# A matmul with batch norm on one core: a raw block and a DMA-turned block more, and the order of the work written out as a table

## Chip, core and metric

The kernel runs on one core of a Trainium2 chip. The metric is the device time of one execution in microseconds. The kernel before takes 205.89 us, the median of three runs (205.88 to 206.04). All times below are microseconds unless they are marked ns. The five engines are PE (TensorE), DVE (VectorE), ACT (ScalarE), POOL (GpSimd) and SP (SyncE, which here only issues DMAs).

## What is computed

```python
y = np.matmul(x, weight)            # x 16 x 512 x 1024, weight 1024 x 768, float32
mean = np.mean(y, axis=(0, 1), keepdims=True)
var = np.var(y, axis=(0, 1), keepdims=True)
y_norm = (y - mean) / np.sqrt(var + eps)
return (gamma * y_norm + beta).astype(np.float32)
```

Each of the 768 output columns is normalized over all 16 x 512 = 8192 rows. No row of a column can be stored before the sums over all 8192 rows of this column are known.

## The kernel before

**Tiling.** The rows form C = 16 chunks of 512 rows, numbered c. The columns form six tiles of 128, numbered nt = 0 to 5. "Fourth tile" is nt = 3, "fifth tile" nt = 4, "sixth tile" nt = 5. The kernel has three stretches.

1. *Loading.* POOL issues DMAs that cast x to bfloat16 (L403). DVE turns the blocks so that the contraction dimension lies on the partitions (turn_x, L428 and L435). PE multiplies each chunk with the first two tiles, rows on the partitions (mm_rows, L510). ACT squares these, DVE and POOL add up sums and squares, ACT keeps the values in bfloat16. For chunks 0 to 3 PE also computes tiles 2 to 5 with the columns on the partitions (mm, L575). Some chunks are copied into a plain layout first (part_chunk, L547), on ACT or, for the last four, ACT or DVE.
2. *Turn-over.* Chunks 14 and 15 of the first two tiles are computed with columns on the partitions (ga_unit, L814). `merges` adds up the accumulators, `sums_rows` (L871) sums them over the partitions on PE, and scale and shift of the first two tiles follow (scale_rows, shift_rows, spread_rows L903). Between the loads and the first store lie "raw turns" (below).
3. *Output.* PE computes tiles 2 to 5 for chunks 4 to 15, tile by tile, while all finished blocks are normalized and stored. A tile's scale and shift come from finish_tasks (L968 to L1017), once all of its chunks have their sums.

**A column block.** Two chunks of one tile, 1024 rows, 512 KB of output. With the columns on the partitions it must be turned before it is stored. There are three ways:

- *pe* (col_block with MODE 'pe'): DVE normalizes it in place (norm, L1026), PE turns it with eight 128x128 transposes into PSUM (turn_block, L1044), ACT copies it to SBUF as float32 (L1210), SP stores it (L1202).
- *xact* (MODE 'xact'): the same norm, then SP issues a DMA that turns it (L1220), ACT converts the result to float32 (L1232), SP stores it (L1202).
- *raw* (RAW): SP turns the values before they are normalized (raw_turn, L1106, into the tile r_sb). When scale and shift are known, raw_spread makes rows of them (a DVE turn at L1142, gather and deal of small copies at L1145, a copy into a PSUM bank at L1158); DVE multiplies (norm_raw, L1174), POOL adds the shift (add_raw, L1178), SP stores (L1182). Raw turns of chunks 0 to 3 need no sums, so they may run ahead of the first store. The first of them waits for the last load of x.

In the kernel before, tile 2 has raw blocks c = 0 and 2 and 'xact' for the rest, the fourth tile raw c = 0 and 'xact' for the rest, the fifth tile raw c = 0, 2 and 4 and 'pe' for the rest. The last block of the fifth tile is held back (held_block, its norm early, its turn, copy L1252 and store L1255 after PE's last column matmul) to fill the time in which the sixth tile's sums are finished.

**The end.** The sixth tile's last chunk is computed in two pieces of 256 columns (last_unit, L753). Then follow the statistics of the last pieces (L760), the aggregate (L1308), the root on ACT (root, L1311) and the affine values on DVE (affine, L1323 and L1324). After them all 8192 rows of the sixth tile are normalized (norm_part, L1348), turned on PE, copied by ACT (L1361) and stored (L1364) in eleven blocks.

**What sets the order.** Every piece of work is a Task with a priority, the engines that may run it with occupation and latency, and what it depends on. arrange (L122 to L224) is a planner: it steps through time, picks the engine that is free first, and gives it the ready task of lowest priority number. A PE turn can be hosted by a matmul task: its transposes are issued between the matmuls. The instructions are emitted in this order and chained on each engine by `seq`, so each engine runs exactly its own sequence. SP too works in order: a store or turn that waits holds up all that are behind it.

negate_gamma (L963) makes -gamma for the scale of tile 2; it is one small DVE instruction (L964), after shift_rows.

Of the kernel before, what the change touches and what calls it, by code (L numbers as in the profile page):

```python
# [97 lines left out]
class Wires:  # L98
# [8 lines left out]
    def ready(self, queue):  # L107
        lanes = self.lanes[queue]
        return 0.0 if len(lanes) < self.LANES else lanes[-self.LANES]
# [9 lines left out]
        return t, land  # L119


def arrange(tasks, turns, log=None):  # L122

    free = {e: 1.25 for e in ("PE", "DVE", "ACT", "POOL", "SP")}
    wires = Wires()
    port = {"DVE": 0.0, "POOL": 0.0}
    left = sorted(tasks, key=lambda t: t.prio)
    order = []  # L130
    SEM, LOOK = 0.06, 0.2

    def ready(t):
        if t.after is not None and t.after.end is None:
            return None
        r = 0.0
        for d in t.deps:
            if d.end is None:
                return None
            r = max(r, d.end + SEM + t.slack)  # L140
        kept = [(s.pool, s.pool.mark()) for s in t.takes] if len(t.takes) > 1 else []
        fits = True
        for s in t.takes:
            p = s.pool.place(s)
            if p is None:
                fits = False
                break
            r = max(r, p[0] + SEM)
            if kept:
                s.pool.take(s, p[1])  # L150
        for pool, mark in reversed(kept):
            pool.reset(mark)
        if not fits:
            return None
        if t.dma:
            r = max(r, wires.ready(list(t.engines)[0]))
        return r

    def start_of(t, r, e):

        b = max(r, free[e])
        if e == "DVE" and t.lock:
            b = max(b, port["POOL"])
        elif e == "POOL" and not t.dma:
            b = max(b, port["DVE"])
        return b

    while left:
        seen = [(t, ready(t)) for t in left]
        first = {}  # L170
        for t, r in seen:
            if r is not None:
                for e in t.engines:
                    b = start_of(t, r, e)
                    if e not in first or b < first[e]:
                        first[e] = b
        if not first:
            raise RuntimeError(f"nothing can begin: {[(t.prio, t.emit) for t in left[:8]]}")
        e = min(first, key=lambda k: first[k])
        best = None  # L180
        for t, r in seen:
            if r is not None and e in t.engines and start_of(t, r, e) <= first[e] + max(LOOK, t.look):
                if best is None or t.prio < best[1]:
                    best = start_of(t, r, e), t.prio, t
        start, _, t = best
        for s in t.takes:
            s.pool.take(s, s.pool.place(s)[1])
        occ, lat = t.engines[e]
        t.hosted = []
        if t.hosts:  # L190
            room = t.hosts
            for u, r in seen:
                if u in turns and r is not None and r <= start + 0.3 and room >= 1:
                    n = min(room, turns[u][0])
                    if turns[u][0] == turns[u][1]:
                        places = [s.pool.place(s) for s in u.takes]
                        if any(p is None or p[0] > start for p in places):
                            continue
                        for s in u.takes:
                            s.pool.take(s, s.pool.place(s)[1])  # L200
                        u.takes_done, u.takes = u.takes, []
                    t.hosted.append((u, n))
                    turns[u][0] -= n
                    room -= n
                    occ += 0.0555 * n
                    lat += 0.0555 * n
        if t in turns:
            occ = lat = 0.0555 * turns[t][0]
            lat += 0.2
            t.count = turns[t][0]  # L210
        free[e] = start + occ
        if e == "DVE" and t.lock or e == "POOL" and not t.dma:
            port[e] = start + occ
        t.end = start + lat
        if t.dma:
            free[e], t.end = wires.send(e, start, occ, t.dma, t.count)
        t.start, t.engine = start, e
        order.append(t)
        left.remove(t)
        for u, n in t.hosted:  # L220
            if turns[u][0] == 0:
                u.end = t.end + 0.2
                left.remove(u)
    return order  # L224


# [1 line left out]
def kernel(  # L228
# [9 lines left out]
    nc = tc.nc  # L238
# [3 lines left out]
    ALU = mybir.AluOpType  # L242
# [5 lines left out]
    P = 128  # L248
# [24 lines left out]
    XT, YB, SQ = C - EARLY, 28, 3  # L273
    ADDED = (0,6,16,28,40)
    PARTED, LATE, SINGLE = (4,5,7,8,9,10), (12,13,14,15), (2,3,6)
    MODE = {2:'xact',3:'xact',4:('pe',)*8}
    MODE = {nt: m if isinstance(m, tuple) else (m,) * (C // GY) for nt, m in MODE.items()}
    RAW, RAWADD, RAWDUE = {2:(0,2),3:(0,),4:(0,2,4)}, {2:'POOL',3:'POOL',4:'POOL'}, {2:14.0,3:8.0,4:8.0}
    RING = 3 * CH // 32 * KQ // 2
    ENG = {"ACT": nc.scalar, "DVE": nc.vector, "POOL": nc.gpsimd, "SP": nc.sync}  # L280

# [11 lines left out]
    def seq(bi):  # L293

        ins = bi.ins
        prev = last.get(ins.engine)
        if prev is not None:
            tc.add_manual_dep(
                ins, prev,
                mybir.DependencyInfo(mybir.DependencyClass.NoSync, mybir.DependencyReason.DATA),  # L300
                reason="order",
            )
        last[ins.engine] = ins.name
        return bi

    gamma_sb = singles.tile([P, NT], f32)
# [28 lines left out]
    ngamma = singles.tile([P, NT], f32)  # L335
# [17 lines left out]
    tasks, turns = [], {}  # L353
    banks, xts, ys, sqs, rings = Pool(8), Pool(XT), Pool(YB), Pool(SQ), Space(RING)

    def task(prio, engines, emit, deps=(), lock=False, **kw):
        t = Task(prio, engines, emit, deps, **kw)
        t.lock = lock
        tasks.append(t)
        return t  # L360

    def dve(occ):
        return {"DVE": (occ, occ + 0.09)}

    def act(occ):
        return {"ACT": (occ, occ + 0.11)}

    def pool(occ):
        return {"POOL": (occ, occ + 0.05)}
# [70 lines left out]
    order = [("x", 0), ("w", 0, 2), ("x", 1), ("w", 2, 4)]  # L440
# [5 lines left out]
    t = 1.0  # L446
    affine = None
# [237 lines left out]
    def y_of(nt, c):  # L685
        return y_col.setdefault((nt, c // GY), Slot(ys))
# [174 lines left out]
    S = clock[0]  # L861
# [61 lines left out]
    sr = task(U + 0.1, dve(0.35), shift_rows, [sc], True)  # L923
# [32 lines left out]
    k = 0  # L956
# [4 lines left out]


    def negate_gamma(eng):  # L963
        seq(nc.vector.tensor_scalar(ngamma, gamma_sb, -1.0, None, op0=ALU.mult))  # L964

    ng = task(S, dve(0.1), negate_gamma, [affine, sr], True)

    def finish_tasks(nt):  # L968
        deps = [col_end[nt, c][0] for c in range(C)]
# [49 lines left out]
    def norm(nt, c, n=1):  # L1019
        def emit(eng):  # L1020
            part = y(nt, c, n)
            if eng == "ACT":
                seq(nc.scalar.activation(
                    part, part, AF.Identity, bias=shift[:, nt:nt + 1], scale=scale[:, nt:nt + 1]))
            else:
                seq(nc.vector.tensor_scalar(  # L1026
                    part, part, scale[:, nt:nt + 1], shift[:, nt:nt + 1],
                    op0=ALU.mult, op1=ALU.add))
        return emit
# [161 lines left out]
    def col_block(nt, c, due, fin_task, held=False):  # L1191
# [12 lines left out]
        a = task(due, act(1.144) if nt == GA else dve(0.45), norm(nt, c, GY), [fin_task] + keeps, nt > GA, uses=[yslot])  # L1204
        if MODE[nt][c // GY] == "pe":
            b, bank = turn_block(due + 0.5, nt, m0, count, [a], [yslot])
# [11 lines left out]
        def xbar(eng):  # L1218
# [3 lines left out]
        b = task(due + 0.5, {"SP": (1.4, 1.4)}, xbar, [a], dma=XBAR,  # L1222
                 takes=[t_slot] + ([slot] if MODE[nt][c // GY] == "xact" else []), uses=[yslot])
        if MODE[nt][c // GY] == "xpool":
            def store_x(eng):
                seq(nc.gpsimd.dma_start(dst(), t_slot.o))
# [41 lines left out]
    for nt in range(GA, NT - 1):  # L1268
# [10 lines left out]
        f = finish_tasks(nt)  # L1279
        start = clock[0] + 3.0  # L1280
# [58 lines left out]
    for c, r0, rows in ends:  # L1339
        due = E + 2.0 + 0.6 * c  # L1340
        n = max(rows // CH, 1)
# [13 lines left out]
        b, bank = turn_block(due + 0.6 * (n - 1), nt, m0, count, norms, [y_of(nt, c + i) for i in range(n)])  # L1355
# [7 lines left out]
        def store(eng, slot=slot, m0=m0, count=count):  # L1363
# [6 lines left out]
             uses=[slot])  # L1370

    order = arrange(tasks, turns)
    if "PLAN" in globals():
        PLAN.append(order)
# [37 lines left out]
```

## Time and profile before

| | |
|---|---|
| median of three runs | 205.89 |
| span of the profiled execution, first to last instruction | 204.1 |
| PE, DVE, ACT, POOL busy | 189.3, 159.3, 146.2, 124.1 |
| HBM read, written | 36.71 MB, 25.17 MB |
| SP's DMA transposes: L1220, L1106 | 13, 6 |
| PE idle between 110 and 187 | none in any window |
| last chunk's last matmul ends | 186.62 |
| sixth tile's affine values done | 188.16 |
| last store issued | 198.56 |

The profile is that of one execution. Its own time is known only as its span, 204.1; the median of the timed runs is 1.8 more, for what lies before the first and after the last instruction. "Busy" is time in which an instruction of the engine runs; starts and lengths are counted from the start of the span. In a group's row the numbers after the bar are busy time, mean ns of one instruction, and the idle time of its engine ahead of it, with what ended that. "DMA" rows give the busy share of the 16 DMA engines in tenths, "GB/s" rows what they moved.

### The profile page before, as it was taken

What the parts mean: (1) busy time and instruction counts of PE and PEld (TensorE: products, weight loads), DVE (VectorE), ACT (ScalarE), POOL (GpSimd) and SP (SyncE); (2) the same over time, 40 slices, a digit from 0 to 9 for tenths busy, and PEclk for the clock granted to TensorE, in tenths of its full rate; (3) what the DMA queues carried; (4) which work ended last, traced back from release to release, by engine and by line L of the source; (5) the groups of instructions that cost most, each with busy time, mean ns of one, the idle gap of its engine ahead of it and who ended that gap; (6) DMA issues with size and microseconds to landing.
All of it is one profiled execution on the core that took longest, in us unless ns stands there. A gap on an engine that the chain in (4) does not pass through costs nothing.

```text
span 204.1 us, 3510 instructions
## 1 busy us (share of the span) xinstructions
PE 189.3 (93%) x1210; PEld 114.5 (56%) x1210; DVE 159.3 (78%) x250; ACT 146.2 (72%) x260; POOL 124.1 (61%) x150
## 2 busy tenths in 40 slices
PE   7969999999999999999999999999999999997900
PEld 3457554657488888777865444444444445544600
DVE  4031879999999999969989998987999878657900
ACT  2001461368989999899978766999998959956950
POOL 7776954877499989997403999389613312940000
PEclk9999999999999999999999999999999999999965
DMA  4999999999999999999686899899999999999998
GB/s 71 172 199 196 176 196 196 196 197 197 190 193 197 197 196 196 196 197 195 103 181 200 297 339 336 248 301 328 295 322 227 336 303 274 347 343 310 310 347 253
DMA packets 98562, 48.74 MB, mean 239 GB/s; under 512 B 24304, under 2 KB 98032, under 8 KB 98544
## 3 DMA queue, kind: packets, MB, share of 16 engines
q0 software_dynamic: 34624, 18.36, 65.5%
q1 hardware_dynamic: 63920, 30.16, 52.6%
q8 instruction: 9, 0.15, 0.3%
q14 instruction: 9, 0.07, 0.1%
HBM read 36.71 MB, written 25.17 MB: 303 GB/s over the span
## 4 chain that ended last, share of the span: by engine, by line
PE 86%; ACT 3%; DMA 3%; POOL 2%; issue 1%; ACTq 0%; DVE 0%; POOLq 0%
PE y_ps L575 54%; PE y_ps L510 24%; PE y_ps L814 4%; ACT o_sb L1361 3%; DMA ring<-in_x_dram 3%; PE o_ps L1044 1%; POOL ring L403 1%; POOL w_sb L387 1%; PE y_ps L753 1%; PE a_ps L903 1%; PE o_ps L1074 0%; ACTq L1407 0%; PE idle_ps L591 0%; PE tot_ps L871 0%; ACT ring L1252 0%
## 5 line engine op out<-in xcount | busy, mean ns | idle before, releaser
L575 PEld LDWEIGHTS <-w_sb 128*128 128x128 bf16 x520 | 50.3, 97 | 57.6
L575 PE MATMUL y_ps<-xT_sb,w_sb 128*128 128x512 bf16 (+1 forms) x272 | 59.3, 371 | 0.0
L575 PE MATMUL y_ps<-x_pl,w_sb 128*128 128x512 bf16 x248 | 57.4, 379 | 0.0
L403 POOL DMA_DIRECT2D ring<-in_x_dram x76 | 47.2, 626 | 14.4 <-DMA ring<-in_x_dram 5.5
L510 PE MATMUL y_ps<-w_sb,xT_sb 128*128 128x256 bf16 x448 | 50.6, 273 | 1.7 <-DMA ring<-in_x_dram 1.6
L510 PEld LDWEIGHTS <-xT_sb 128*128 128x128 bf16 x448 | 43.5, 98 | 9.4 <-DVE xT_sb L435 2.9
L435 DVE STREAM_TRANSPOSE xT_sb<-ring 128x1024 f32<-128x1024 f32 (+1 forms) x29 | 31.2, 1111 | 14.1 <-DMA ring<-in_x_dram 13.9
L711 DVE BATCH_NORM_STATS2 stats<-y_ps 128x6 f32<-128x512 f32 x46 | 30.9, 687 | 7.7 <-PE y_ps L575 7.2
L715 ACT CAST y_sb<-y_ps 128x512 bf16<-128x512 f32 x51 | 29.0, 593 | 10.4 <-DVE stats L711 6.3
L547 ACT COPY x_pl<-xT_sb 128x1024 bf16<-128x1024 bf16 x32 | 32.8, 1063 | 1.7 <-DVE xT_sb L435 1.7
L942 POOL TENSOR_TENSOR ring<-ring,sum 128x1024 f32<-128x1024 f32 (+1 forms) x11 | 23.8, 2188 | 14.9 <-ACT y_ps L724 10.9
L659 ACT ACTIVATE sq_sb<-y_ps 128x512 f32<-128x512 f32 x28 | 16.3, 610 | 16.2 <-PE y_ps L510 15.9
L666 POOL TENSOR_TENSOR sum<-sum,sq_sb 128x512 f32<-128x512 f32 x20 | 25.6, 1278 | 3.0 <-ACT sq_sb L659 1.7
L662 DVE TENSOR_TENSOR sum<-y_ps,sum 128x512 f32<-128x512 f32 x28 | 18.9, 675 | 6.3 <-ACT sq_sb L659 5.3
L672 ACT CAST y_sb<-y_ps 128x512 bf16<-128x512 f32 x28 | 16.3, 594 | 8.2 <-DVE sum L662 8.0
L1178 POOL TENSOR_TENSOR ring<-ring,sum 128x1024 f32<-128x1024 f32 x6 | 14.8, 2477 | 9.8 <-issue 8.5
L937 DVE TENSOR_TENSOR ring<-y_sb,a_ps 128x1024 f32<-128x1024 bf16 (+1 forms) x16 | 16.7, 1079 | 0.1
L1044 PE MATMUL o_ps<-ident,y_sb 128*128 128x128 bf16 x104 | 13.1, 221 | 1.6 <-DVE y_sb L1348 1.5
L1232 ACT CAST ring<-ring 128x1024 f32<-128x1024 bf16 x13 | 13.8, 1063 | 0.6 <-DMA ring<-y_sb 0.6
L1145 POOL COPY sum<-sum 32x256 f32<-32x256 f32 (+1 forms) x17 | 5.8, 340 | 13.4 <-DVE sum L1142 6.5
L428 DVE STREAM_TRANSPOSE xT_sb<-ring 128x2048 bf16<-128x2048 bf16 x6 | 13.5, 2290 | 0.1
L591 PE MATMUL idle_ps<-idle_sb 128*128 128x512 f32 x18 | 9.6, 688 | 1.5 <-DVE idle_sb L316 1.5
(104 smaller groups left out, 153.7 us busy)
## 6 DMA issues: line engine op xcount, KB each, us to landing
out_dram<-ring SPq DMA_DIRECT2D x37, 512.0 KB, 3.4
ring<-in_x_dram POOLq DMA_DIRECT2D x52, 256.0 KB, 8.8
out_dram<-o_sb SPq DMA_DIRECT2D x6, 512.0 KB, 4.7
ring<-in_x_dram POOLq DMA_DIRECT2D x16, 128.0 KB, 5.9
w_sb<-in_weight_dram POOLq DMA_DIRECT2D x8, 192.0 KB, 6.2
out_dram<-ring SPq DMA_DIRECT2D x6, 256.0 KB, 3.0
ring<-in_x_dram POOLq DMA_DIRECT2D x4, 192.0 KB, 7.8
out_dram<-o_sb SPq DMA_DIRECT2D x3, 256.0 KB, 2.5
```

What stands on the lines that cost most here:

```text
L403: bi = seq(nc.gpsimd.dma_start(x_bf[32 * i:32 * i + 32], src[:, :, KQ * i:KQ * (i + 1)]))
L435: seq(nc.vector.transpose(dst, src[:, :, jw0:jw1]))
L510: seq(nc.tensor.matmul(y_ps[:, s], x_of(c, jw, e, t * P, (t + 1) * P), w_sb[:, jw, e, 0:NA], start=(s == 0 and jw == 0 and e == 0), stop=( ...
L547: seq(nc.scalar.copy(dst, pairs) if eng == "ACT" else ENG[eng].tensor_copy(dst, pairs))
L575: seq(nc.tensor.matmul(y_ps, w_sb[:, jw, e, nt * P:(nt + 1) * P], moving(c, jw, e, q0 * QR, q1 * QR, parted), start=(jw == 0 and e == 0 an ...
L659: seq(nc.scalar.activation(sq_sb[:, 0:n], slot.tile[:, 0:n], AF.Square))
L662: seq(nc.vector.tensor_add(sum1, slot.tile[:, 0:n], sum1))
L666: seq(ENG[eng].tensor_add(acc, acc, state["sq"][:, 0:n]))
L711: seq(nc.vector.bn_stats(dst, slot.tile))
L715: seq(nc.scalar.copy(y(nt, c), slot.tile))
L937: seq(nc.vector.tensor_mul(slot.o, y_row[c].y[:, s0:s1], aff[0][:, None, :].to_broadcast([P, n, NA])))
L942: seq(ENG[eng].tensor_add(slot.o, slot.o, row[:, None, :].to_broadcast([P, n, NA])))
```

## The change

- The fourth tile's block c = 2 becomes raw: its turn moves from behind its norm to the group of raw turns ahead of the first store, and it is finished by a DVE product and a POOL add in place of a norm and an ACT convert.
- The fifth tile's block c = 8 becomes 'xact' instead of 'pe': the DMA turns it, and ACT converts it from SBUF instead of copying it from PSUM.
- negate_gamma goes from DVE to POOL and no longer waits for shift_rows.
- arrange no longer chooses. It takes task and engine from a table, ORDER: a letter for the engine (P, V, A, G, S for PE, DVE, ACT, POOL, SP) and the number of the task in the order of the calls of task(). A rider after "+" is a turn and the number of its transposes that this matmul hosts. Dependencies and buffer places are found as before.

The table keeps the order of the first part up to about the last rows of x. From there on it differs widely. Tasks that the prediction names: 53, 55, 56 and 58 are turns of the last rows of x; 299 and 296 bn of ga_unit; 381 negate_gamma, 320 to 322 the merges, 323 sums_rows; 313 the ga_unit that needs the rows of 56 and 58; 392 to 397 the raw turns ahead of the first store; 386 the ga store; 677 and 678 chunk 5 of the sixth tile, 632 to 637 the last chunks of the fifth; 662 the DMA turn of c = 8; 666 and 670 the PE turns of c = 10 and 12; 607 the cast of c = 7, 642 the fifth tile's root; 725 the sixth tile's root, 731 and 734 the held copies, 746 the first final copy (c = 1, 512 rows).

In the table PE often begins a second chunk before the first one's second half: in the fifth tile at most four are begun and not ended.

```diff
+ORDER = (
...
+    "V282 A279 V288 A284 V287 P411 A291 P412 V52 A289 G293 P413 A263 P416 P295 P298 G320 G381 G321 G322 V292 "
+    "V53 V319 V299 V296 A264 A294 A402 A414 A297 A408 A415 A300 A403 P304 P323 P301 V55 V58 V56 P307 P313 "
+    "P310 V308 V305 V324 V314 V302 V311 A309 P316 V325 V317 V326 A303 A312 A306 A315 A327 A318 A409 V328 P417 "
+    "P420 P330 V329 V382 V383 V388 V387 V336 V339 V345 P331 P421 P384 S394 S393 S392 S397 S395 S396 A332 A418 "
...
+    "A530 S380 S466 P592 P593 P600 P612 P597 P608 P616 P601 P617 P609 P620 P613 V582 V594 V541 V552 V583 V560 "
...
+    "S640 S561 S569 S559 S551 P621 P604 P605 P624 P677 P625 P678 P632 P628 P633 P629 P636 P637 P673 P674 V606 "
...
+    "P685+658.4 P686+658.1,666.2 P682+658.3 V691 V669 V651 V683 A659 A684 A663 A692 S548 S575 S660 P693+666.1 "
+    "P706 P697 P694+666.1 P698+666.1,670.1 P701+670.2 P702+666.3,670.1 G652 S653 S664 V654 V729 V687 V707 "
...
+    "V711 V721 V723 V715 V718 V724 V726 A704 A671 A712 A716 A725 A731 V728 V744 V753 V748 V752 P745 P749 P754 "
+    "A734 A722 A746 A750 A755 A719 S656 S650 S668 S672 S732 S735 S747 S751 V767 V757 V777 V758 V763 V773 V736 "
...
+)
 def arrange(tasks, turns, log=None):
...
-    left = sorted(tasks, key=lambda t: t.prio)
+    left = tasks
...
-        start, _, t = best
+    NAMES = {"P": "PE", "V": "DVE", "A": "ACT", "G": "POOL", "S": "SP"}
+    for word in ORDER.split():
+        word, _, riders = word.partition("+")
+        t, e = left[int(word[1:])], NAMES[word[0]]
+        r = ready(t)
...
+        for rider in riders.split(",") if riders else ():
+            i, n = rider.split(".")
+            u, n = left[int(i)], int(n)
...
-    MODE = {2:'xact',3:'xact',4:('pe',)*8}
+    MODE = {2:'xact',3:'xact',4:('pe','pe','pe','pe','xact','pe','pe','pe')}
...
-    RAW, RAWADD, RAWDUE = {2:(0,2),3:(0,),4:(0,2,4)}, {2:'POOL',3:'POOL',4:'POOL'}, {2:14.0,3:8.0,4:8.0}
+    RAW, RAWADD, RAWDUE = {2:(0, 2),3:(0, 2),4:(0, 2, 4)}, {2:'POOL',3:'POOL',4:'POOL'}, {2:14.0,3:8.0,4:8.0}
...
     def negate_gamma(eng):
-        seq(nc.vector.tensor_scalar(ngamma, gamma_sb, -1.0, None, op0=ALU.mult))
-
-    ng = task(S, dve(0.1), negate_gamma, [affine, sr], True)
+        seq(nc.gpsimd.tensor_scalar(ngamma, gamma_sb, -1.0, None, op0=ALU.mult))
+
+    ng = task(S, pool(0.3), negate_gamma, [affine])
```

More of the change, by code (lines that the diff above doesn't have):

```diff
@@ L128, in arrange @@
     port = {"DVE": 0.0, "POOL": 0.0}
-    left = sorted(tasks, key=lambda t: t.prio)
+    left = tasks
     order = []
-    SEM, LOOK = 0.06, 0.2
+    SEM = 0.06
     def ready(t):
@@ L166, in start_of @@
         return b
[L168 to L184, printed above, removed]
-        start, _, t = best
+    NAMES = {"P": "PE", "V": "DVE", "A": "ACT", "G": "POOL", "S": "SP"}
[3 more added lines that the diff above has]
+        r = ready(t)
+        if r is None:
+            raise RuntimeError(f"out of order: {word}")
+        start = start_of(t, r, e)
         for s in t.takes:
@@ L189, in arrange @@
         t.hosted = []
[L190 to L206, printed above, removed]
+        for rider in riders.split(",") if riders else ():
+            i, n = rider.split(".")
+            u, n = left[int(i)], int(n)
+            if turns[u][0] == turns[u][1]:
+                for s in u.takes:
+                    s.pool.take(s, s.pool.place(s)[1])
+                u.takes_done, u.takes = u.takes, []
+            t.hosted.append((u, n))
+            turns[u][0] -= n
+            occ += 0.0555 * n
+            lat += 0.0555 * n
         if t in turns:
@@ L218, in arrange @@
         order.append(t)
-        left.remove(t)
         for u, n in t.hosted:
@@ L222, in arrange @@
                 u.end = t.end + 0.2
-                left.remove(u)
     return order
```

28 rows, old and new, of the table ORDER are left out of this document.

## The prediction

> **What bounds the kernel now.** I read part 1 of the page first. TensorE is busy for 93% of the span, more than any other engine:
>
> ```profile
> PE 189.3 (93%) x1210; PEld 114.5 (56%) x1210; DVE 159.3 (78%) x250; ACT 146.2 (72%) x260; POOL 124.1 (61%) x150
> ```
>
> A share over the whole span hides stages, so the table by windows came second (length, busy time of PE, PEld, DVE, ACT and POOL, clock, DMA share, GB/s):
>
> ```profile
> 140.00:150.00 10.00, 10.00 (x48) 4.46 (x46) 9.69 (x18) 10.00 (x15) 6.29 (x3) 1.00 1.12 309
> 178.00:187.00 9.00, 9.00 (x56) 4.87 (x53) 5.89 (x11) 4.69 (x9) 2.76 (x2) 1.00 1.15 345
> 187.00:196.00 9.00, 5.53 (x66) 3.61 (x64) 6.33 (x22) 8.49 (x15) 0.00 (x0) 0.98 1.02 305
> 196.00:204.10 8.10, 0.00 (x0) 0.00 (x0) 0.00 (x0) 0.67 (x2) 0.00 (x0) 0.50 0.95 287
> ```
>
> PE has no idle time up to 187, at full clock, though ACT or DVE is nearly full beside it. After 187 the DMA carries the end. The chain of waits, in order of time, shows the handover (start, length, what):
>
> ```profile
> 169.34 0.06 PE o_ps L1044
> 169.40 0.22 PE y_ps L575
> 169.61 0.06 PE o_ps L1044
> ...
> 184.80 1.81 PE y_ps L753 x16
> 186.62 0.24 PE o_ps L1044 x4
> ...
> 186.92 0.58 ACT ring L1252
> 187.51 0.20 ACT std L1311
> ...
> 187.93 0.23 DVE fss L1324
> ...
> 188.19 0.36 DVE y_sb L1348
> ```
>
> The last matmul ends at 186.62, the held block's copy (L1252) at 187.50, the last affine at 188.16. Only then can the sixth column tile, 4.19 MB, be normalized and stored. Whether older stores still hold it up is read from the DMA view of 186 to 194, in 40 slices of 0.2 us:
>
> ```profile
> DMA  9999999994216999699968949949999999999999
> GB/s 343 341 353 340 353 343 353 343 353 118 84 44 207 323 348 338 195 346 346 351 200 269 338 131 330 266 138 340 346 351 338 343 351 346 343 346 351 346 351 346
> ```
>
> The rate falls at 187.8: older stores are through. Held data comes at about 188.4, 0.9 after its copy ended. Dips follow until 191.4, then the rate is flat at some 345. Added up against 345, the dips after 188.4 lose about 0.5 us. So the end is PE's work, a fixed chain, and 4.72 MB (held block and sixth tile) at 345 GB/s, or 13.7 us.
>
> **The change part by part.** The groups give the durations (last: mean ns, idle):
>
> ```profile
> L1178 POOL TENSOR_TENSOR ring<-ring,sum 128x1024 f32<-128x1024 f32 x6 | 14.8, 2477 | 9.8 <-issue 8.5 <-DVE ring L1174 1.3
> L1232 ACT CAST ring<-ring 128x1024 f32<-128x1024 bf16 x13 | 13.8, 1063 | 0.6 <-DMA ring<-y_sb 0.6
> L1210 ACT CAST ring<-o_ps 128x1024 f32<-128x1024 bf16 x4 | 4.0, 1014 | 0.2 <-DMA out_dram<-ring 0.2
> L1174 DVE TENSOR_TENSOR ring<-r_sb,a_ps 128x1024 f32<-128x1024 bf16 x6 | 7.3, 1214 | 1.8 <-DMA out_dram<-ring 1.8
> ```
>
> *PE.* Block c=8 of the fifth tile loses its eight PE turns. In the chain a matmul with a turn beside it takes 0.27 us (169.34 to 169.61), and eight without turns 1.73, 0.216 each: 0.056 per turn, 0.45 us for eight. PE does nothing else less or more. Since PE never idles, this is on the path: **-0.45**.
>
> *ACT.* Block c=8 is converted from SBUF (1.063) instead of copied from PSUM (1.014): +0.05. Fourth-tile block c=2 loses a convert: -1.06. The table gives ACT ten of the sixteen plain copies (L547), where the profile has eight: 2 x 1.08. It gives the fifth tile's four gathers (0.24 each) to POOL: -0.97. Net +0.2 of 146; hidden by ACT's idle after 150 (8.72 busy in 150 to 160). If that cover failed, 0.2.
>
> *DVE.* Minus a norm (L1026, 0.54), plus a two-input product (1.21), minus two plain copies (0.72 each), minus the negation (0.16): -0.9, off the path.
>
> *POOL.* Plus an add (2.48), four gathers (0.23 each) and the negation. POOL is idle for 6.0, 6.5 and 6.3 us before its groups at 152.3, 161.4 and 170.2, which hides add and gathers. The negation lies between the merge and the additions that sums_rows waits for. POOL has no 128x6 row; its 128x1 copy takes 0.18, its 128x256 additions 0.8 (1.61 for two). I take 0.2, nearest to the small one. Additions then end at 99.5 instead of 99.33. PE comes there at 99.43 in both, since one unit is exchanged, so 0 to 0.1, and up to 0.7 by the large one. I take 0.1.
>
> *SP and DMA.* Bytes stay. Twenty transposes instead of nineteen, of them six instead of five ahead of the first store and fourteen behind it in both (fourth-tile c=2 goes, fifth-tile c=8 comes). Five took SP 6.86 us from 100.08, 1.37 each, so the sixth ends at 108.3. The table's first store waits for the ga copy, which ends at 109.28 (ACT L1082, 108.27 + 1.01). The DMA view of 100 to 110 moves nothing from about 108.3 on; the transfer falls into that hole. Cost 0; behind the store it would be 1.4 us of SP, hidden by the stream's reserve below.
>
> *Order.* Three places touch the path. (a) Turn 58 of the last rows now precedes 56, and a bn (0.42) precedes both. DVE's three turns ended at 101.40 and will at 101.8; PE reaches the first unit that needs them, third-last instead of second-last, after two more units, 100.24 + 2 x 0.91 = 102.06. Cost 0; whatever they are later than 102.06 is lost one for one. (b) Two halves of sixth-tile chunk 5 now precede the end of the fifth tile's sums, so its affine comes 1.75 later, at 167.9 instead of 166.15. The c=8 transpose on SP waits for it and two norms, until some 170, with two finished fourth-tile stores queued behind. What covers this: older data must be out by the start of held data. The spread-out PE turns end with the last older block at 181.8 (back from 186.2 by 0.91, 1.73, 0.91, 0.86), ACT's casts and copy at 184, so its 1.5 us of data are out by about 186.5, 2 us in time. Moreover DVE no longer puts the product and add of one rows block (0.68 and 0.69) ahead of POOL's first norm, so POOL's adds can start 1.4 us earlier than 110.46. (c) In the tail the root now precedes the held copies on ACT. All times move by -0.45 + 0.1 = -0.35: the root ends at 187.35 instead of 187.70, the affine at 187.8 instead of 188.16. But the held copy, 0.58, starts only when the root is nearly done, some 187.25, and ends at 187.85 instead of 187.50; its data starts 0.9 later, at 188.75 instead of 188.4. That is 0.35 back. The first final block is now 512 columns wide instead of 256: norm 0.41, turns 0.41, cast 0.62, seams 0.1, so its copy ends at 189.35 and its data can start at 190.25, just when the held block's 1.5 us are over. So the dips of the old tail, 0.5, can go.
>
> **The sum.** Old tail: 188.4 + 13.7 + 0.5 = 202.6. New tail: 188.75 + 13.7 = 202.45, when the stream has no dip. That is -0.15; PE's -0.45 is inside it, since an affine 0.45 later would open a dip of that size. If the held copy's end comes 0.2 earlier, as it would if no stall of 0.1 occurs and the copy overlaps the root by 0.2, it is -0.35. Both ends are near; I take **-0.25**. The profiled execution has a span of 204.1 and the median is 205.89; the 1.8 between them shows in no row, and I keep it: 205.89 - 0.25 = 205.64, say **205.6**. The best end, with PE's whole 0.45 passed on and the held copy no later than PE allows (187.50 - 0.45), is 205.89 - 0.45 - 0.5 = 204.9; the other end, held data 0.35 later and the dips kept, is 206.2.
>
> **The rivals.**
>
> *The tail keeps the whole gain of PE (faster).* If the held copies get ahead of the root, or their data starts sooner than 0.9 after them because the queue is empty, the tail moves by PE's 0.45 and loses some of its dips: 205.3. For it: 0.9 holds SP's 0.37 for the issue, and 0.5 beyond it is the only such seam I have. Against: ACT works in order.
>
> *PSUM banks run out (slower).* Before, one accumulation at most is half done when another unit starts; the table holds up to four open in the fifth tile (c=9, 8, 10 and 6), while banks are eight and a spread row holds one. A finished unit needs its bn (0.69) and cast (0.59) to free a bank, and the table puts casts behind converts and the root, for example c=7 behind the fifth tile's root. Each time PE finds no bank it waits about 1.3 us. One such wait gives -0.25 + 1.3: 206.9; two give 208.2. It decides from 0.7 us of new PE idle in 110 to 187. Against it: four open and two in eviction leave one or two. [...]
>
> *PE's busy time hides waits that the order removes (faster by more).* The 269 matmuls of 110.40 to 169.34 take 58.94 us, 0.219 each, against 0.216 in the fastest run: at most 0.8 us, giving 204.8. It is weak, as strided operands explain the difference as well. [...]
>
> *The older stores run late.* If a hole of the DMA like that of 172.6 to 173.4 (0.8 us) falls after 184, the 2 us reserve still covers it; two and a wait for c=8 do not, and 205.9 to 206.5 results.
>
> **How the numbers follow.** Forecast, with small stalls of PE (two late turns or sums of 0.2 to 0.3) among it: 0.38, 205.5 to 206.2. Whole gain 0.24, 205.1 to 205.48. Banks 0.22. Hidden waits 0.05. Late stores 0.11, half of them above 206.3. A measurement here tells 0.2%, 0.41 us, from no change. Faster, below 205.48: 0.24 + 0.05 = 0.29, and 0.02 of the forecast's edge, 0.31. Slower, above 206.3: 0.22 + 0.05 and 0.02 of the forecast's other edge, 0.29. Same: 0.40. The range takes in forecast, whole gain, late stores and one bank wait: 205.1 to 206.9, leaving out hidden waits, every term at its best, and two bank waits.
>
> **What would show it.** PE turns x96 instead of x104, none idle in 110 to 187 and its last column matmul (L753 or L575) ending at 186.2 to 186.3; r_sb transposes x7, six before 109; affine by 187.8; held data from 188.75, and no dip in the DMA rate from there to 202.45. Wrong if PE idles by over 0.4 us, if the DMA still drains older blocks at 188.7, or if turns 56 and 58 end after 102.1.

## Result and the profile after

The changed kernel takes 206.81 us (median of 14 executions, 205.82 to 207.02); the kernel before, run beside it, 205.91 (14 executions, 205.56 to 206.30). The ratio is 1.0029, with a 95% interval of 1.0016 to 1.0042: slower by 0.90 us between the medians, where 0.25 less was forecast. By the ratio it is 0.60, since the fourteen times fall into two groups, eight at 206.79 to 207.02 and six at 205.82 to 206.39. Lines of the kernel's body stand 24 further down than before: L1044 is now L1068, L1348 L1372, L1361 L1385, L1364 L1388, L1407 L1431.

Part 1 of the page and the table by windows, in the same columns as before:

```profile
PE 190.1 (93%) x1187; PEld 116.3 (57%) x1202; DVE 156.8 (76%) x247; ACT 145.6 (71%) x257; POOL 128.4 (63%) x156
```

```profile
140.00:150.00 10.00, 9.95 (x47) 4.51 (x46) 8.50 (x16) 8.97 (x14) 7.21 (x6) 1.00 1.15 319
178.00:187.00 9.00, 8.68 (x61) 5.10 (x60) 6.70 (x14) 5.55 (x9) 4.09 (x2) 1.00 1.09 325
187.00:196.00 9.00, 6.26 (x58) 5.01 (x59) 6.02 (x21) 7.06 (x12) 0.00 (x0) 0.65 1.01 305
196.00:205.00 9.00, 0.83 (x9) 0.66 (x7) 0.00 (x0) 2.89 (x5) 0.00 (x0) 0.69 0.84 252
```

Up to PE's last column matmul little has changed. The 0.05 that PE lacks in the first window are matmul records missing from the trace (1187, where e1_tail_old with the same order up to there has 1202 and no gap on PE from 110 to 184). The last two rows have changed. Between 187 and 196 the granted clock is 0.65 instead of 0.98, and after 196 PE still runs nine turns and ACT five copies, where before PE ran nothing and ACT two. The chain of waits says what was waited for:

```profile
187.85 3.57 DVE y_sb L1372 x11
191.43 0.32 DVEq L1431
191.75 1.56 DVE y_sb L1372 x5
193.31 0.05 issue
193.35 2.54 PE o_ps L1068 x22
195.89 0.02 issue
195.92 1.29 ACT o_sb L1385 x2
```

The end now goes through all of DVE's norms, to 193.31, and then through 22 turns, whose starts are 0.107 apart (0.056 at the full clock of the profile before). In the old chain DVE's norms were on the path for 0.36, and from 189.60 on it ran through ACT's copies alone:

```profile
188.19 0.36 DVE y_sb L1348
...
189.60 4.74 ACT o_sb L1361 x6
```

The DMA view of 186 to 204, in 40 slices of 0.45 us, shows what this does to the stores; first the kernel before, then the changed one:

```profile
GB/s 341 350 348 348 95 180 339 277 348 250 237 217 345 343 349 343 349 346 346 346 352 343 349 347 347 345 347 348 344 348 349 346 346 347 349 343 347 32 0 0
```

```profile
GB/s 340 347 347 324 44 23 257 345 347 328 352 340 344 277 346 348 344 348 352 345 347 349 346 250 348 347 325 132 208 336 326 346 349 344 348 347 350 341 76 0
```

The old dips (250, 237, 217 at 190 to 191.4) are gone, as forecast. A new hole stands at 198.2 to 199.1 (132, 208).

One more difference lies behind the last store. The waits on SP's queue (total, times, longest) for the end of the program, of the kernel before and of the changed one:

```profile
SPq L1407 <- DMA out_dram<-o_sb: 2.8, 3, 1.5
```

```profile
SPq L1431 <- DMA out_dram<-o_sb: 2.9, 1, 2.9
```

Before, three waits were ended one by one by stores that landed; now a single wait lasts until a landing. The instructions on that line from just before the last landing on (x3 and x10: number; then min/median/max ns and first and last start) of the two kernels:

```profile
L1407 SPq EVENT_SEMAPHORE  x3: 17/17/28, 203.2 to 204.0; - x3
```

```profile
L1431 SPq EVENT_SEMAPHORE  x10: 17/28/28, 203.7 to 204.9; - x10
```

Before, one such wait and the two of the closing barrier follow the last landing (203.15); now eight and the two (landing 203.65). They are about 0.062 apart (0.059 to 0.065 in the changed kernel's trace).

Taken apart at two points that the trace gives, the end of the last column matmul (E) and the landing of the last store (L), the profiled executions of all kernels compare like this (medians are those of each kernel's own runs):

| kernel | SP DMAs | E | E to L | L to end | median |
|---|---|---|---|---|---|
| before | 88 | 186.62 | 16.53 | 0.92 | 205.91 |
| changed | 89 | 186.28 | 17.37 | 1.35 | 206.81 |
| e1_tail_old | 89 | 186.36 | 16.63 | 1.35 | 206.04 |
| e2_one_turn | 89 | 185.71 | 16.71 | 1.34 | 206.04 |
| e3_warm | 89 | 185.84 | 17.06 | 1.35 | 206.24 |
| e4_blocks_planner | 89 | 185.75 | 20.52 | 1.34 | 209.84 |
| e5_before_89 | 89 | 186.37 | 16.55 | 1.35 | 206.31 |
| e6_after_88 | 88 | 186.90 | 17.54 | 0.91 | 206.15 |
| e7_one_turn_88 | 88 | 185.50 | 16.70 | 0.92 | 205.62 |
| e8_before_tail_of_after | 88 | 186.58 | 17.36 | 0.91 | 206.40 |
| e9_old_tail_88 | 88 | 186.23 | 16.61 | 0.92 | 205.54 |
| e10_held_first_88 | 88 | 185.96 | 16.70 | 0.91 | 205.74 |
| e11_raw_planner | 88 | 186.66 | 18.79 | 0.91 | 207.84 |
| e12_dma_turn_planner | 89 | 186.29 | 18.19 | 1.34 | 207.36 |

E differs between executions of one order (185.50 to 186.90 for the changed kernel and those that share its order up to there), so single spans say less than the two other columns. Kernels with the same tail agree there to about 0.1, but for e6_after_88, where the older stores ran late (see there).

### The profile page after: what moved, and what is told of

Read it like the earlier page. It is cut to its first block, busy times and chain, and to the rows that moved or that the text cites. A ratio compares the mean times of both kernels' runs of the same rounds, so it can differ in the third digit from the quotient of the medians.

```text
span 205.0 us, 3472 instructions
## 1 busy us (share of the span) xinstructions
PE 190.1 (93%) x1187; PEld 116.3 (57%) x1202; DVE 156.8 (76%) x247; ACT 145.6 (71%) x257; POOL 128.4 (63%) x156
## 4 chain that ended last, share of the span: by engine, by line
PE 79%; DMA 9%; DVE 4%; POOL 2%; ACT 1%; issue 1%; DVEq 0%; ACTq 0%; POOLq 0%
PE y_ps L599 50%; PE y_ps L534 21%; DMA w_sb<-in_weight_dram 6%; PE y_ps L838 4%; DMA ring<-in_x_dram 3%; DVE y_sb L1372 3%; PE o_ps L1068 2%; ACT o_sb L1385 1%; POOL ring L427 1%; PE y_ps L777 1%; POOL w_sb L411 1%; DVE xT_sb L459 1%; PE a_ps L927 1%; PE o_ps L1098 0%; PE tot_ps L895 0%
## 5 line engine op out<-in xcount | busy, mean ns | idle before, releaser
L599 PE MATMUL y_ps<-xT_sb,w_sb 128*128 128x512 bf16 (+1 forms) x264 | 59.9, 371 | 0.5
L571 ACT COPY x_pl<-xT_sb 128x1024 bf16<-128x1024 bf16 x34 | 34.7, 1057 | 2.3 <-DVE xT_sb L459 1.7
L735 DVE BATCH_NORM_STATS2 stats<-y_ps 128x6 f32<-128x512 f32 x46 | 30.0, 683 | 6.1 <-PE y_ps L599 6.1
L1202 POOL TENSOR_TENSOR ring<-ring,sum 128x1024 f32<-128x1024 f32 x7 | 16.8, 2401 | 8.6 <-issue 7.9
L1068 PE MATMUL o_ps<-ident,y_sb 128*128 128x128 bf16 x96 | 12.9, 264 | 3.1 <-ACT ring L1276 1.6
L1169 POOL COPY sum<-sum 32x64 f32<-32x64 f32 (+1 forms) x21 | 7.2, 344 | 10.4 <-DVE sum L1166 9.6
L1068 PEld LDWEIGHTS <-y_sb 128*128 128x128 bf16 x96 | 8.5, 120 | 5.3 <-DVE y_sb L1372 4.3
```

The source lines that it names most:

```text
L571: seq(nc.scalar.copy(dst, pairs) if eng == "ACT" else ENG[eng].tensor_copy(dst, pairs))
L599: seq(nc.tensor.matmul(y_ps, w_sb[:, jw, e, nt * P:(nt + 1) * P], moving(c, jw, e, q0 * QR, q1 * QR, parted), start=(jw == 0 and e == 0 an ...
L735: seq(nc.vector.bn_stats(dst, slot.tile))
L1068: seq(nc.tensor.transpose(dst, src, ident))
L1202: seq(ENG[eng].tensor_add(slot.o, slot.o, row[:, None, :].to_broadcast([P, n, P])))
```

## The experiments

The theories at the start: T1, the order of the table behind the sixth tile's affine values makes the hole; T2, the halved clock makes it; T3, the loss comes from the new blocks or the order ahead of the tail. T4, the waits at the end, was formed after the first four runs.

**e1_tail_old: the tail in the old order (T1).** Only the words of the table behind the affine values change, to the order that the kernel before has:

```diff
-V744 V753 V748 V752 P745 P749 P754
...
-V736 V768 V778 V772 V762 V782 V740 P759 A760 S756 S761 P769 P741 P764 P783 P779 P737 P774
...
+V736 V740 P737 A738 S739 P741 A742 S743 V744 P745 A746 S747 V748 P749 A750 S751 V752 V753 P754 A755 S756
...
```

> The changed kernel with the old order of everything behind the sixth tile's affine values: norms, turns, copies and stores block by block, rows 0 to 511 first. The rest of the table is kept, the root ahead of the held copies too. Theory 1 (the tail's order: the turn of rows 256 to 511 waits on PE for DVE's very last norm, and 22 turns of four other blocks stand behind it): the hole in the stores goes, 205.4 to 205.7, in all runs, also where the clock is halved, since eight turns at half clock take 0.9 and a store 1.5. Theory 2 (the granted clock, halved from 189.75 on in the profile, is the cause, whatever the order): the clock is halved as often as before and the time stays at 206.5 to 206.9 in those runs. Theory 3 (the new blocks or the order ahead of the tail cost it): 206.5 to 206.9.

Measured: 206.04, ratio to before 1.0006 (0.9993 to 1.0019). The same DMA view:

```profile
GB/s 360 336 342 348 109 22 196 347 345 344 341 339 346 346 344 348 346 350 341 350 348 344 348 348 345 347 350 347 345 347 347 345 347 348 345 347 255 0 0 0
```

No hole, no dip from 189.2 to the end, and 0.77 less than the changed kernel. So the order of the tail costs that much; but the result only equals before, 0.4 above what the prediction's sum would give. T1 is not all.

**e2_one_turn: one turn moved.** In the changed order the PE turns of rows 256 to 511 (741), which need DVE's very last norm (740), stand ahead of five others whose norms come before it. Turn and copy move behind them:

```diff
-P769 P741 P764 P783 P779 P737 P774 A770 A765 A780 A742 A738 A784 A775
+P769 P764 P783 P779 P737 P774 P741 A770 A765 A780 A738 A784 A775 A742
```

> The changed kernel with one block put elsewhere: the PE turn and the ACT copy of the sixth tile's rows 256 to 511 go behind those of all other blocks; its norm is the last and its store the last in both. The scattered order of the norms stays. Theory 1 in its narrow form (this one wait is the cause): 205.5 to 205.9. If the scattered norms cost as much as the one wait, 206.1 to 206.5. Theories 2 and 3: 206.5 to 206.9.

Measured: 206.04, ratio 1.0006 (0.9993 to 1.0019), between the two ranges that T1 was given, and the same as e1_tail_old. E to L is 16.71 instead of 17.37, so this one place decides nearly all that the tail loses. The profiled execution had the full clock in the tail (1.00 from 187 to 196), the changed kernel's not (0.65); but that of e7_one_turn_88 below, with the same order and a mean clock of 0.975 where e2 has 0.985, has the same E to L (16.70).

**e3_warm: PE kept busy (T2).** Fourteen matmuls whose result nobody reads, ahead of and between the turns of the tail (6, 1, 1, 3 and 3 behind tasks 752, 749, 754, 759 and 769), order unchanged.

> The changed kernel, its order kept, with fourteen additional matmuls of 512 columns on PE where it is idle in the tail (six ahead of the first final turn, then 1, 1, 3 and 3 between the turns), whose result nobody reads. Theory 2: the clock stays at 1.00 to the end of the turns, and the time is 205.5 to 205.9 with little spread. Theory 1: the clock stays up too, but the last five blocks still wait for the last norm; 22 turns take 1.2 instead of 2.5, so about half of the hole goes and the time is 205.9 to 206.4. Theory 3: 206.5 to 206.9.

Measured: 206.24, ratio 1.0020 (1.0009 to 1.0032). The windows of the tail:

```profile
187.00:196.00 9.00, 6.70 (x75) 4.44 (x73) 5.78 (x19) 7.83 (x13) 0.00 (x0) 1.00 1.10 332
196.00:204.00 8.00, 0.00 (x0) 0.00 (x0) 0.00 (x0) 1.57 (x3) 0.00 (x0) 0.60 0.90 270
```

The clock is full from 187 to 196 and PE is through by 196. E to L is 17.06: 0.3 less than changed, 0.4 to 0.5 more than with the old order. By this profile the late turn costs at full clock too, and the halved clock adds to it. The medians give the clock more: e3_warm takes back 0.57 of the 0.77 that the old order takes back. What the added matmuls cost by themselves isn't shown, since no run has them with the old order. So T2 is not ruled out as a part of the loss; the next part comes back to it.

**e4_blocks_planner: the blocks without the table (T3).** The kernel before with RAW, MODE and the negation of the change, ordered by its planner.

> The kernel before with the new blocks alone: the fourth tile's c = 2 raw, the fifth tile's c = 8 turned by the DMA, the negation on POOL; the planner sets the order. Theories 1 and 2: PE's 0.45 arrives with the old tail, 205.4 to 205.7. Theory 3, if it is the blocks: 206.3 to 206.9; if it is the order ahead of the tail, 205.4 to 205.9.

Measured: 209.84, ratio 1.0195 (1.0173 to 1.0216). From 187 to 204 the DMA has no idle slice, since older stores drain until 193.41 (before 189.53). One reason stands in the timeline:

```profile
186.51 2.34 POOL L1178 TENSOR_TENSOR ring<-ring,sum 128x1024 f32<-128x1024 f32 x1 [3.47 <-DVE ring L1174]
188.88 0.37 SPq L1182 DMA_DIRECT2D out_dram<-ring  x1
```

A raw block's addition ends at 188.85, behind PE's last column matmul, and its store is issued only then. With the table the last older store landed at 189.10.

**e5_before_89 and e6_after_88: the waits at the end (T4).** The trace records which semaphore each DMA of SP raises. In those of the kernel before and of the changed one eight are used in turn: 108, 110, 112, 113, 115, 116, 117 and 118, eleven times over. At the end SP waits for them in this order in both: in the changed kernel's trace the waits start from 203.67 (108) to 204.10 (118), in that of the kernel before from 199.98 to 203.17. The change adds a turn by the DMA, 89 instead of 88, so the last store raises the semaphore that is waited for first (108) instead of last (118). e5 makes the 89 in the kernel before, by loading gamma with six small DMAs instead of five at about 49 us; e6 makes the 88 in the changed kernel, by loading it with four. The diffs of the one and the other:

```diff
-            n = 2 if nt < 2 * PAIRED else 1
+            n = 2 if nt < 0 else 1
```

```diff
-            n = 2 if nt < 2 * PAIRED else 1
+            n = 2 if nt < 4 else 1
```

> The kernel before with one small load more on SP: the first two of gamma's columns are loaded by two DMAs instead of one, at about 49 us, where SP and its queue have nothing else to do. Nothing else differs on any engine. SP then issues 89 DMAs as the changed kernel does, instead of 88. New theory, T4: each DMA of SP takes the next of eight semaphores in turn, and at the end SP waits for the eight one after another, about 0.062 us a wait, in a fixed order. With 88 the last store has the semaphore that is waited for last (one wait behind its landing at 203.15, end 0.92 after it); with 89 it has the first, and seven more waits come behind its landing (changed kernel: landing 203.65, span 205.00, 1.35 after it). T4: 0.43 us slower than before, about 206.35, ratio 1.002; the last landing stays at 203.15 or thereabouts and the span ends 1.35 behind it. If the whole loss came from the order of the tail (T1) or the clock (T2): the same as before, 205.9.

Measured: 206.31, ratio 1.0041 (1.0019 to 1.0063). Seven of the eleven times lie at 205.94 to 206.39, four at 207.14 to 208.47, for which no run shows a reason.

```profile
SPq L1407 <- DMA out_dram<-o_sb: 3.0, 1, 3.0
```

```profile
L1407 SPq EVENT_SEMAPHORE  x10: 17/28/28, 202.9 to 204.2; - x10
```

The stores land as before (E to L 16.55), and the row of ten waits appears, with the end 1.35 behind the landing.

> The changed kernel with one small load fewer on SP: the second two of gamma's columns are loaded by one DMA instead of two, at about 49 us. SP issues 88 DMAs. T4: 0.43 us faster than the changed kernel, about 206.4, still about 0.45 above before because the hole in the tail is left; the span ends 0.92 behind the last landing. T1 or T2 alone: 206.8, as the changed kernel.

Measured: 206.15, ratio 1.0009 (0.9993 to 1.0024), 0.25 below the 206.4 expected; against the changed kernel's 206.81, which ran in another group, 0.66 less. The two ratios, 1.0029 and 1.0009, are 0.41 us apart. The profiled execution ran late: E is at 186.90, and the last older store landed at 190.81 instead of 189.10. Its DMA view has no hole at 198, and its mean clock is 0.978 where the changed kernel's is 0.971, so its span and its E to L say nothing of the changed tail. The end is 0.91 behind the landing.

**e7_one_turn_88: both repairs.** e2_one_turn with the edit of e6.

> The changed kernel with both repairs: turn 741 and copy 742 moved as in e2_one_turn, and 88 DMAs on SP as in e6_after_88. If the loss is the sum of the hole in the tail (0.5 to 0.8) and the seven waits (0.43), this comes to e2_one_turn's 206.04 less 0.43, 205.6, that is 0.3 below before, ratio about 0.9985: what the prediction's sum had for the change, 205.6. If the waits don't count: 206.0.

Measured: 205.62, ratio 0.9996 (0.9984 to 1.0008); 0.42 below e2_one_turn, as the end's share of 0.43 would have it. The two ran in different groups, though, and their ratios, 1.0006 and 0.9996, are only 0.21 apart; those of e1_tail_old and e9_old_tail_88 below are 0.49 apart. That it is faster than before isn't shown.

**e8_before_tail_of_after: the new tail in the kernel before.** Old blocks, old order as a table (on every engine the same instructions in the same order as the planner gave), and behind the affine values the new order.

> The kernel before, its order written out as a table word for word (the same instructions on every engine), and only the final blocks behind the affine in the order that the changed kernel has; blocks, modes and the 88 DMAs of SP are those of before. T1: the hole of 0.5 to 0.8 us opens in the stores of the tail here too, 206.4 to 206.7, with the last landing about 203.7. T4 alone: the same as before, 205.9. T3 (the new blocks ahead of the tail): the same as before.

Measured: 206.40, ratio 1.0028 (1.0015 to 1.0041). The DMA view has the dip again (224, 234, 207 at 198.2 to 199.5), and E to L is 17.36:

```profile
GB/s 346 346 347 340 83 201 339 274 344 51 259 345 347 265 348 349 348 344 348 347 345 347 348 320 252 347 350 224 234 207 327 344 348 348 344 348 349 345 301 1
```

So the tail's loss needs nothing of the rest of the change. The landing came at 203.94, where 203.7 was expected. T3 falls for the changed kernel.

**e9_old_tail_88: the change without its two losses.** e1_tail_old with the edit of e6.

> The changed kernel with the old order of the tail, as in e1_tail_old, and 88 DMAs of SP, as in e6_after_88. T1 and T4 together: 206.04 less 0.43, 205.6, ratio to before about 0.998 to 0.9985, which is the sum of the prediction (205.6); the stream without a hole up to its end, the span's end 0.92 behind the last landing. If more of the change costs time (T3): 206.0.

Measured: 205.54 against 205.78 for before, ratio 0.9982 (0.9965 to 1.0000). This is the fastest median of all, and the interval just reaches no change.

**e10_held_first_88: the root's place.** e9 with `A725 A731` as `A731 A725`.

> e9_old_tail_88 with one pair of ScalarE instructions exchanged: the first copy of the held block is put ahead of the root again, as in the kernel before. The prediction gave 0.35 to this exchange (the held blocks' data 0.35 earlier or later against the affine). If what starts the stream sets the end: the affine comes about 0.3 later, the first held store a little earlier, the last landing the same or up to 0.3 later: 205.6 to 205.9. If the root's place sets the end, 0.3 slower than e9_old_tail_88; if the first held store sets it, up to 0.3 faster.

Measured: 205.74, ratio 0.9990 (0.9978 to 1.0002); against e9 within the spread. In the trace the first held store is issued 1.10 after E, against 1.58 in e9, and E to L is 16.70 against 16.61. Half a microsecond in the place of the held data moves the last landing by 0.1.

**e11_raw_planner and e12_dma_turn_planner: each block alone, ordered by the planner.** Only the line RAW, or only the line MODE, changes; the negation stays on DVE.

> The kernel before, its order still by its planner, with only the raw block of the fourth tile more (RAW of tile 3 (0, 2)), negation on VectorE as before. It has 88 DMAs of SP. e4_blocks_planner, with both blocks, took 209.84, of which the waits at the end are 0.43. If the raw block's additions, late on POOL and VectorE in the planner's order, are what delays the older stores: +2.5 to +3.5, 208.4 to 209.4. If it is the other block: 205.9.

Measured: 207.84, ratio 1.0094 (1.0075 to 1.0114); older stores land until 191.83. The groups' row shows POOL's additions waiting for 15.1 us in all for DVE's products, where in the kernel before it was 1.3:

```profile
L1178 POOL TENSOR_TENSOR ring<-ring,sum 128x1024 f32<-128x1024 f32 x7 | 17.3, 2477 | 17.4 <-DVE ring L1174 15.1 <-issue 2.3
```

> The kernel before, its order still by its planner, with only the one block of the fifth tile turned by the DMA instead of PE. It has 89 DMAs of SP, so 0.43 comes from the waits at the end (T4). If the raw block is what costs in e4_blocks_planner: 205.4 to 206.4 (0.45 of PE's work less, which may or may not count, plus 0.43). If this block is: 208 to 209.5.

Measured: 207.36, ratio 1.0074 (1.0055 to 1.0094); older stores land until 190.87. Neither expectation of one guilty block held: 2.06 and 1.58 together make 3.64 of the 3.9 of e4. Each block delays the older stores, and 0.43 of e12 are the waits at the end. Another part lies at the end of the stores: the DMA views end with 173 and 57 GB/s in e11 (up to 204, the last landing at 205.45), with 52, 26 and 22 in e12 (landing at 204.48), in slices of 0.45, and with 161 and 12 in e4, in slices of 1.45. The kernel before and the changed one go from 347 and 341 to nothing with one slice between. So the older stores alone do not make the whole loss. Why the stores end so unevenly isn't shown, and which queue holds the older stores up in e12 was not taken further.

## Why the prediction was wrong

**What held.** *PE*: 96 turns, no idle time, and the last matmul at 186.28 (forecast 186.2 to 186.3). Over the eight profiled executions that have the table's order up to there, E is 186.10 on the mean, over the three with the old one 186.52: -0.42, against -0.45 plus 0.1 for POOL. The eight lie between 185.50 and 186.90, so this mean is good to some 0.2, by an estimate from their spread. *POOL*: the negation took 0.241 (0.2 taken). *Order (a)*: DVE's three turns ended at 102.02, forecast 101.8 against 102.06 needed, and no stall followed. *Order (b)*: the rate fell at 187.8, not at 186.5, so 1.3 of the reserve of 2 was used; still ahead of the held data. *Order (c), its first part*: affine at 187.81 (187.8), first final copy issued for store at 189.37 (copy's end forecast 189.35), dips of 190 to 191.4 gone. The rival of the banks (eight in the kernel's PSUM pool) didn't come: PE has no new gap. For the rival of hidden waits: in the profile before, L575's matmuls start 0.225 apart when they read xT_sb and 0.216 when they read the plain copies (medians of those without a turn between), 0.219 on the mean of all, so the operands explain its difference as well. Older stores were not late with the table; e4, e11 and e12 show that they would be without it. Off the path the sums were further off: DVE's busy time fell by 2.5 (0.9 forecast), ACT's by 0.6 (0.2 more forecast).

**What failed, first: "the dips can go" and "no dip in the DMA rate from there to 202.45".** The step followed the new tail to its first final block and took the rest of the stream for flat. The order of the table was there to be read: norms 736 and 740 come late, 740 last of all; turn 741, which needs it, comes ahead of 764, 783, 779, 737 and 774. PE runs them in this order (the first turn behind DVE's end at 193.31 starts at 193.35), and ACT and the stores wait behind the 32 turns that are then left. The step also took PE's turns at full clock, as in the one profile of the kernel before (0.41 for the first block); in the changed kernel's profile those 32 ran at half clock up to 196.58. E to L grows by 0.84 (16.53 to 17.37); e8, the kernel before with the new tail, has 0.83 of it, and e2 gets back 0.66 by moving one turn.

**Second: "SP and DMA ... Cost 0".** The step counted twenty transposes instead of nineteen and priced their bytes and SP's time. It did not ask what the count itself decides: which semaphore the last store raises. Seven waits at 0.062 come behind it, 0.43 us: the end is 1.34 or 1.35 behind the landing in every kernel with 89 DMAs and 0.91 or 0.92 in every one with 88.

**The sum.** -0.42 at E, +0.84 in the tail, +0.43 at the end: +0.85, against 0.90 between the medians and 0.60 by the ratio; that the first two agree so closely is more than the spread of E warrants. Without the two losses (e9) the medians differ by -0.24, where the sum had -0.25. By the ratio it is -0.37. That is partly luck: the sum's 0.35 for the held data and 0.5 for the dips are not two independent terms. In e10 the held data came 0.5 earlier and the landing moved 0.1 the other way. What e9's interval leaves open is whether the tail keeps PE's whole gain (205.3) or part of it (205.6).

**What stays open.** How the tail's loss divides between order and clock. At full clock the new tail costs 0.4 to 0.5 by the profile of e3, 0.2 by its median, and 0 to 0.2 by the timed executions with a mean clock of 0.984 or more: 206.04 on the mean for the changed kernel, which is e1's median; 205.55 for e6, where e9 has 205.54; 206.02 for e8, where before has 205.81. In those at 0.978 or less the same three are 0.7 above e1, e9 and before. So by this split most of the loss needs both, the late turn and the halved clock. The kernel before loses nothing at 0.978 or less (figures in the last section), so it is the order that lets the clock count: 32 turns behind the last norm, 0.107 instead of 0.056 apart, are 1.6 us of PE time more, by estimate, with the stores waiting behind them.

## What to carry to other kernels

Where stores set the end, follow an order to its last block, not to its first: one instruction that needs another engine's last result holds up all that stand behind it in its engine's sequence, though their data is ready (here turn 741, 0.66). Count the DMAs of a queue when an edit adds one, and look behind the last landing: what the program still waits for there is on the path whole (here 0.43). A profile is one execution with one course of the clock; where the timed executions fall into groups, look at the clock of each. And when an edit comes with a new order, try each in the other's place (here the new tail in the old kernel, and the new blocks with the old planner), since one can hide what the other costs.

## What the runs showed of the hardware

**In two traces the halved clock followed stretches in which PE was busy for about half or less.** In the changed kernel's trace the granted clock is 1.0 up to 189.75, 0.5 from there, 1.0 from 196.58 and 0.5 from 200.00: steps 6.83 and 3.41 apart. In that of the kernel before it is 1.0 up to 195.67 and 0.5 from there. In stretches as long as the shortest of these, 3.41, counted from the steps, PE's busy share was:

| kernel | stretch | PE busy | clock in it | clock behind it |
|---|---|---|---|---|
| changed | 186.34 to 189.75 | 0.46 | 1.0 | 0.5 |
| changed | 189.75 to 193.17 | 0.71 | 0.5 | 0.5 |
| changed | 193.17 to 196.58 | 0.95 | 0.5 | 1.0 |
| changed | 196.58 to 200.00 | 0.07 | 1.0 | 0.5 |
| before | 185.43 to 188.84 | 0.55 | 1.0 | 1.0 |
| before | 188.84 to 192.26 | 0.99 | 1.0 | 1.0 |
| before | 192.26 to 195.67 | 0.54 | 1.0 | 0.5 |

A share of 0.55 was followed by the full clock and one of 0.54 by the halved one, so these traces show no share that decides. PE's pause ahead of the final turns, 1.60 in the changed kernel and 1.53 in the kernel before, lies in the stretch of 0.46 in the one and of 0.55 in the other. That its place decides whether the clock is halved in the tail is not shown, since no run moves the pause alone: e1_tail_old had 1.00 from 187 to 196 and a mean of 0.986, and e9_old_tail_88, with the same instructions on PE, a mean of 0.974.

**Executions with a lower mean clock were longer where PE's turns are late, and not in the kernel before.** In e9 the mean clock of the profiled execution was 0.974 and E to L is 16.61; in e1 it was 0.986 and it is 16.63. Of the profiled executions with a mean clock of 0.984 or more, e1_tail_old, e2_one_turn and e3_warm had 1.00 from 187 to 196; of those with 0.978 or less, the changed kernel (0.971) had 0.65 there and e8 (0.973) 0.69. For the timed executions the mean alone is known, not where the clock was halved. By this split the executions of the kernel before took 205.88 on the mean at 0.984 or more (41) and 205.89 at 0.978 or less (30). The changed kernel took 206.04 (four) and 206.75 (ten, one of them as short as 205.99), e6 205.55 (three) and 206.26 (eight), e8 206.02 (four) and 206.50 (five). With the one turn moved the split is not settled: 205.77 (four) and 206.20 (seven) in e2, 205.70 (four) and 205.68 (eight) in e7.

**The waits for DMAs that had landed were not free**: in the changed kernel's trace they start 0.059 to 0.065 after one another, seven of them behind the one that the last landing ended.
